# A one-column product written as a scalar-tensor-tensor operation, and a row minimum that starts from the sink's column

## The chip, the cores and the metric

The kernel runs on one core of one Trainium2 chip. The core has five engines that work side by side and wait for one another through semaphores: TensorE (PE in the profile, its weight loads PEld), VectorE (DVE), ScalarE (ACT), GpSimd (POOL), and SyncE (SP), which here only issues DMA transfers. The metric is the device time of one execution in microseconds (us); lower is better. Each engine carries out its own list of instructions in order.

## The reference

One layer of a decoder: RMSNorm, two attention branches side by side, gates, a residual, a second RMSNorm, a gated MLP with a width-3 causal convolution, a residual and a last RMSNorm, on 1024 tokens of 1024 channels, all in float32. The two branches matter here.

The first is differential attention with 4 heads. Each head has two query/key components of 64 channels, and the result uses the difference of two softmaxes:

```python
logits = s - slopes[:, None, None, None] * dist
logits = jnp.where(dist >= 0, logits, NEG_INF)
p = jax.nn.softmax(logits, axis=-1)
a = p[:, :, 0] - lam * p[:, :, 1]
return jnp.einsum('bhqs,bshe->bqhe', a, v)
```

The second is sliding-window attention, 8 heads in 2 groups, a window of 128, in which each head has a learned sink: one more logit that takes part in the softmax and has no value behind it:

```python
p = jax.nn.softmax(jnp.concatenate([logits, sink], axis=-1), axis=-1)[..., :-1]
o = jnp.einsum('bnkgqs,bnskd->bnqkgd', p, vw)
```

## The kernel before, in words

Activations lie transposed, with channels on the 128 partitions and tokens in the free dimension. Most products are made to float32 accuracy from three passes: a float32 operand is split into a high and a low part, and TensorE adds high x high, high x low and low x high into one PSUM bank. `mm3` (lines 150 to 152) and `product` (835 to 837) are those passes; the splits are copies on ScalarE and subtractions on VectorE (lines 129 and 131 for weights, 755 and 756 for activations).

The stages follow one another: `project` (all input projections, up to about 250 us), `attention` (to about 500 us), `rest` (gates, the merging of the branches, `mix`), `hidden` (the up projection and the convolution) and `down`.

`attention` has six units `u`. Units 0 to 3 are the heads of the differential attention, each of 8 blocks of 128 queries (`da_step`); units 4 and 5 are the two groups of the sliding window, each of 8 blocks for four heads at once (`sw_step`). Between the blocks stand `back_half` calls: half a gate projection each, 24 matmuls of 512 columns that depend on nothing in the attention (lines 150 to 152 and the copy on line 497). They fill TensorE while a softmax is on its way.

A block of the first kind does, for each of two components: scores on TensorE (line 568) into PSUM; on VectorE one operation that adds the bias, scales, writes the negated logits and keeps their minimum along the row (line 572, shown in the profile as CUSTOM_DVE_ANT_0, followed by a DVE_READ_ACCUMULATOR2_ANT that writes the minimum out); on ScalarE the exponential with that minimum as bias and the row sum as second output (line 573). Then the reciprocal of one sum (576), a product of one column (577), the combination of the two components (578), transposes of the result on TensorE (584), their copy to a high part (586, ScalarE) and a low part (587, VectorE), and the product with the values (596 to 598).

A block of the second kind does, for four heads: scores (656), the bias-scale-minimum operation for each head (659), the minimum of the four columns with the four negated sinks (661), the sum with the sinks (662) and its exponential (663), four exponentials of the scores with the minimum as bias (665), the addition of the sink's term (666), the reciprocal (667), the scaling of the four heads (670: three on VectorE, the fourth on GpSimd), transposes (677), the split (680 and 681), the product with the values (687), and a copy and two additions (689 and 694) before the store.

After the attention `rest` reads the stored results back (`yr`, line 712), splits them (755 and 756) and multiplies them with the output weights of the branches; these are the first products that need everything from the attention.

The order of the instructions on each engine isn't written out by hand. A list scheduler of the framework puts every engine's instructions in order, by its own estimate of what each costs and of when its inputs are there. A changed instruction can therefore move others, on all engines.

The calls that the change touches are in `da_step` and `sw_step`. The column `self.neglam` is minus lambda, `self.nsink` holds the eight negated sinks, and `self.s0` the row sums of the first component.

Of the kernel before, what the change touches and what calls it, by code (L numbers as in the profile page):

```python
# [13 lines left out]
ALU = mybir.AluOpType  # L14
# [28 lines left out]
class Trunk:  # L43
# [510 lines left out]
    def da_step(self, h, i, st, aT):  # L554
        nc, ap = self.nc, self.ap
        q, k = st
        slope = 4.0 ** -(h + 1)
        w = (i + 1) * P

        lo = P if w == 640 else 0  # L560
        cuts = ((0, 256),) if i == 0 else ((0, w),) if w <= H2 else ((0, H2 - lo), (H2 - lo, w))
        pr = []
        for c in range(2):
            sc = self.tl(self.psS, [P, T], "sc")
            qs = q[c][:, i * P:(i + 1) * P]
            for part in range(2):
                for n0, n1 in cuts:
                    nc.tensor.matmul(sc[:, lo + n0:lo + n1], qs, k[c][part][:, n0:n1], start=part == 0, stop=part == 1)  # L568
            L = self.tl(ap, [P, T], "L", bufs=4)
            s = self.tl(self.st, [P, 4], "sm", bufs=8)  # L570
            o = 896 - i * P
            nc.vector.tensor_tensor_reduce(L[:, :w], sc[:, lo:lo + w], self.bias[:, o:o + w], slope, 3e38, ALU.add, ALU.min, s[:, 0:1])  # L572
            nc.scalar.activation(L[:, :w], L[:, :w], AF.Exp, bias=s[:, 0:1], scale=-1.0, accum_out=s[:, 1:2] if c else self.s0[:, i:i + 1])  # L573
            pr.append(L)

        nc.vector.reciprocal(s[:, 2:3], s[:, 1:2])
        nc.vector.tensor_scalar(s[:, 3:4], self.s0[:, i:i + 1], s[:, 2:3], self.neglam, ALU.mult, ALU.mult)
        nc.vector.scalar_tensor_tensor(pr[0][:, :w], pr[1][:, :w], s[:, 3:4], pr[0][:, :w], ALU.mult, ALU.add)
        qo = (i % 2) * P
        for j0 in range(0, i + 1, 4):  # L580
            nj = min(4, i + 1 - j0)
            ps = self.tl(self.psT, [P, 4, P], "t")
            for j in range(nj):
                nc.tensor.transpose(ps[:, j, :], pr[0][:, (j0 + j) * P:(j0 + j + 1) * P], self.ident)
            hi, lo = aT[j0 // 4, 0], aT[j0 // 4, 1]
            nc.scalar.copy(hi[:, :nj, qo:qo + P], ps[:, :nj, :])
            nc.vector.tensor_tensor(lo[:, :nj, qo:qo + P], ps[:, :nj, :], hi[:, :nj, qo:qo + P].bitcast(F32), ALU.subtract)
# [57 lines left out]
    def sw_step(self, g, n, st):  # L645
        nc, ap = self.nc, self.ap
        q, k = st
        k0 = max(n - 1, 0) * P
        w = P if n == 0 else 256
        bo = T + (P if n == 0 else 0)  # L650
        sc = self.tl(self.psS, [P, 4, 256], "sc")
        s = self.tl(self.st, [P, 4, 4], "sw", bufs=4)
        L = self.tl(ap, [P, 4, 256], "L", bufs=4)
        for h in range(4):
            for part in range(2):
                nc.tensor.matmul(sc[:, h, :], q[h][:, n * P:(n + 1) * P], k[part][:, k0:k0 + 256], start=part == 0, stop=part == 1)
        for h in range(4):
            slope = 2.0 ** -(4 * g + h + 1)
            nc.vector.tensor_tensor_reduce(L[:, h, :w], sc[:, h, :w], self.bias[:, bo:bo + w], slope, 3e38, ALU.add, ALU.min, s[:, 0, h:h + 1])
        sink = self.vecs[:, C_SINK + 4 * g:C_SINK + 4 * g + 4]  # L660
        nc.vector.tensor_tensor(s[:, 0, :], s[:, 0, :], self.nsink[:, 4 * g:4 * g + 4], ALU.min)
        nc.vector.tensor_tensor(s[:, 1, :], s[:, 0, :], sink, ALU.add)
        nc.scalar.activation(s[:, 1, :], s[:, 1, :], AF.Exp)
        for h in range(4):
            nc.scalar.activation(L[:, h, :w], L[:, h, :w], AF.Exp, bias=s[:, 0, h:h + 1], scale=-1.0, accum_out=s[:, 2, h:h + 1])
        nc.vector.tensor_tensor(s[:, 2, :], s[:, 2, :], s[:, 1, :], ALU.add)
        self.last = nc.vector.reciprocal(s[:, 3, :], s[:, 2, :])
        for h in range(4):
            eng = nc.gpsimd if h in (3,) else nc.vector
            eng.tensor_scalar(L[:, h, :w], L[:, h, :w], s[:, 3, h:h + 1], None, ALU.mult)  # L670
        po = self.tl(self.psT, [P, H2], "t")
        nblk = w // P
        parts = []
        for b in range(nblk):
            ps = self.tl(self.psT, [P, 4, P], "t")
            for h in range(4):
                nc.tensor.transpose(ps[:, h, :], L[:, h, b * P:(b + 1) * P], self.ident)
            pt = self.tl(ap, [P, 2, 4, P], "aT", F32R, bufs=5)
            hi, lo = pt[:, 0], pt[:, 1]
            nc.scalar.copy(hi, ps)  # L680
            nc.vector.tensor_tensor(lo, ps, hi.bitcast(F32), ALU.subtract)
            parts.append((hi, lo))
        for b, (hi, lo) in enumerate(parts):
            kb = k0 // P + b
            va = self.vsw[kb // 4][:, kb % 4, g]
            for m, pt in enumerate((hi, lo)):
                nc.tensor.matmul(po, va, pt, start=b == 0 and m == 0, stop=b == nblk - 1 and m == 1)
        t = self.tl(self.gpool, [P, 4, P], "g", bufs=2)[0:64]
        nc.scalar.copy(t, po[64:128].rearrange("p (h q) -> p h q", h=4))
        pv = po[0:64].rearrange("p (c e q) -> p c e q", c=2, e=2)  # L690
        tv = t.rearrange("p (c e) q -> p c e q", e=2)
        y = self.tl(ap, [P, 2, P], "ys", bufs=3)
        for e in range(2):
            nc.vector.tensor_tensor(y[64 * e:64 * e + 64], pv[:, :, e], tv[:, :, e], ALU.add)
        self.store(self.yd[4 + 2 * g:6 + 2 * g, :, n * P:(n + 1) * P].rearrange("c p q -> p c q"), y)
# [515 lines left out]
```

## Time and profile before

| quantity | value |
|---|---|
| median of 3 runs | 1355.06 us (1354.48 to 1355.87) |
| profiled execution | 1356.2 us, of which the span of instructions 1354.3 us |
| TensorE busy | 1335.0 us, 99% of the span |
| VectorE busy | 1009.8 us, 75% |
| ScalarE busy | 603.9 us, 45% |
| GpSimd busy | 483.1 us, 36% |
| mean granted TensorE clock | 0.996 |

The profile is taken by the hardware profiler in one execution. Its page gives the busy time of each engine, the span in 40 slices, the chain of work that ended last, and groups of instructions by line with their mean duration and the idle time ahead of them. Other views are cut from the same execution: the waits (who waited for whom and for how long), a table of stretches of the span, and the timeline, in which a row is a start, a duration, an engine, a line, an operation, its output and inputs, and in square brackets the idle time ahead of it with what ended it. Matmuls are pipelined: each is shown for longer than the distance to the next, so a TensorE that is shown as busy isn't proof of full speed. The waits of the weight loads (PEld) show short stops better.

### The profile page before, as it was taken

To read this page: it belongs to the slowest core of one execution; us is meant where nothing else is said; L and a number is where in the kernel's file an instruction comes from. 1 tells how busy PE (TensorE), PEld (TensorE's weight loads), DVE (VectorE), ACT (ScalarE), POOL (GpSimd) and SP (SyncE) were. 2 spreads that over 40 slices of the span, in tenths; PEclk is the share of its full clock that TensorE was granted. 3 is DMA by queue.
4 is the path that set the end of the run, shared out by engine and by line. 5 is a ranking of instruction groups with operands and counts; after the bars stand their busy time and mean duration, and the time that the engine had idled before them with its cause. 6 is when DMAs were issued, how large, how long until landed. Compare 5 with 4: busy or idle time off the path is not lost.

```text
span 1354.3 us, 17160 instructions
## 1 busy us (share of the span) xinstructions
PE 1335.0 (99%) x6304; PEld 1103.6 (81%) x6304; DVE 1009.8 (75%) x1454; ACT 603.9 (45%) x942; POOL 483.1 (36%) x350
## 2 busy tenths in 40 slices
PE   7999999999999999999999999999999999999997
PEld 6888888888887777878888888888888888888886
DVE  8846775388898875355689888888888898986454
ACT  8422232376667664334444334433443345433343
POOL 0436651010102125741455565555555611231011
PEclk9999999999999999999999999999999999999999
DMA  6334443966554235334422222122212248651342
GB/s 255 140 113 164 143 156 114 272 174 175 156 133 144 77 116 219 117 119 136 166 82 88 71 91 94 62 79 93 93 63 83 92 141 311 215 177 64 94 134 85
DMA packets 62470, 179.50 MB, mean 133 GB/s; under 512 B 6833, under 2 KB 15153, under 8 KB 62385
## 3 DMA queue, kind: packets, MB, share of 16 engines
q1 hardware_dynamic: 50928, 160.98, 36.7%
q10 hardware_dynamic: 11456, 17.41, 3.5%
q8 instruction: 50, 0.82, 0.2%
q14 instruction: 36, 0.29, 0.1%
HBM read 129.61 MB, written 48.76 MB: 132 GB/s over the span
## 4 chain that ended last, share of the span: by engine, by line
PE 62%; DVE 17%; POOL 7%; issue 7%; DMA 4%; ACT 3%; POOLq 0%; DVEq 0%; SPq 0%; ACTq 0%
PE t L836 7%; PE t L837 7%; PE t L835 7%; POOL us L965 3%; PE y L996 3%; PE d L996 3%; PE sc L568 3%; PE g L150 2%; PE g L151 2%; DVE c L958 2%; PE g L152 2%; DVE wl L112 2%; DMA gr<-gd 2%; PE sc L151 2%; PE sc L152 2%
## 5 line engine op out<-in xcount | busy, mean ns | idle before, releaser
L970 ACT ACTIVATE c<-us,vecs 128x1024 f32<-128x1024 f32 x44 | 54.8, 1248 | 163.2 <-POOL us L965 160.0
L965 POOL TENSOR_TENSOR us<-us,rstd 128x1024 f32<-128x1024 f32 x42 | 100.7, 2414 | 52.8 <-DVE wl L131 34.3
L110 ACT CAST sh<-sf 128x1024 fp32r<-128x1024 f32 x62 | 64.9, 1051 | 106.2 <-POOL sf L97 61.8
L129 ACT CAST wh<-raw 128x1024 fp32r<-128x1024 f32 (+2 forms) x60 | 60.7, 1012 | 104.8 <-PE sc L151 33.1
L971 DVE SCALAR_TENSOR_TENSOR c<-us,vecs,c 128x1024 f32<-128x1024 f32 x44 | 67.1, 1527 | 51.9 <-ACT c L970 51.9
L131 DVE TENSOR_TENSOR wl<-raw,wh 128x1024 fp32r<-128x1024 f32 (+2 forms) x60 | 75.3, 1256 | 39.1 <-ACT wh L129 29.3
L96 POOL TENSOR_TENSOR sf<-rv 128x512 f32<-128x512 f32 x30 | 42.5, 1417 | 166.7 <-DMA rv<-in_w_up 73.2
L112 DVE TENSOR_TENSOR sl<-sf,sh 128x1024 fp32r<-128x1024 f32 x62 | 88.3, 1426 | 8.2 <-ACT sh L110 8.2
L167 POOL TENSOR_TENSOR rs<-ms,mhalf 128x8 f32<-128x8 f32 (+2 forms) x9 | 14.5, 1614 | 159.1 <-DVE ms L165 148.5
L150 PE MATMUL g<-xh,wh 128*128 128x512 f32 x176 | 70.7, 402 | 0.1
L152 PE MATMUL g<-xh,wl 128*128 128x512 f32 x176 | 70.4, 400 | 0.0
L151 PE MATMUL g<-xl,wh 128*128 128x512 f32 x176 | 70.4, 400 | 0.0
L98 POOL TENSOR_TENSOR sf<-raw,rv 128x512 f32<-128x512 f32 x30 | 41.6, 1386 | 59.9 <-DVE sl L112 59.9
L572 DVE CUSTOM_DVE_ANT_0 L<-sc,bias 128x128 f32<-128x128 f32 (+7 forms) x64 | 47.7, 752 | 17.4 <-PE sc L568 14.1
L551 POOL MEMSET aT<- 128x128 f32 x32 | 6.1, 204 | 152.0 <-PE t L597 101.6
L573 ACT ACTIVATE L<-L,sm 128x128 f32<-128x128 f32 (+7 forms) x64 | 49.6, 778 | 20.7 <-DVE sm L572 18.2
L97 POOL TENSOR_TENSOR sf<-sf,raw 128x512 f32<-128x512 f32 x31 | 58.0, 1870 | 1.6
L972 DVE SCALAR_TENSOR_TENSOR c<-us,vecs,c 128x1024 f32<-128x1024 f32 x44 | 56.2, 1279 | 0.6
L725 POOL TENSOR_TENSOR gr<-gr,rstd 128x1024 f32<-128x1024 f32 x16 | 39.4, 2467 | 41.4 <-DMA gr<-gd 41.2
L112 DVE TENSOR_TENSOR wl<-raw,wh 128x1024 fp32r<-128x1024 f32 (+1 forms) x35 | 52.8, 1508 | 0.1
L151 PE MATMUL sc<-ml,wh 128*128 128x512 f32 x128 | 50.1, 391 | 0.6 <-DVE ml L746 0.6
L568 PE MATMUL sc<-u,u 128*128 128x512 f32 (+2 forms) x192 | 49.8, 359 | 0.1
(444 smaller groups left out, 4351.4 us busy)
## 6 DMA issues: line engine op xcount, KB each, us to landing
u<-qd SPq DMA_DIRECT2D x72, 256.0 KB, 6.1
raw<-in_w_down SPq DMA_DIRECT2D x27, 512.0 KB, 3.7
raw<-in_w_in SPq DMA_DIRECT2D x25, 512.0 KB, 4.4
hr<-hd SPq DMA_DIRECT2D x50, 256.0 KB, 5.3
raw<-in_w_up SPq DMA_DIRECT2D x23, 512.0 KB, 3.6
hd<-c SPq DMA_DIRECT2D x22, 512.0 KB, 2.8
rv<-in_w_up SPq DMA_DIRECT2D x21, 512.0 KB, 3.5
gr<-gd SPq DMA_DIRECT2D x16, 512.0 KB, 3.6
```

What stands on the lines that cost most here:

```text
L112: nc.vector.tensor_tensor(lo, src, hi.bitcast(F32), ALU.subtract)
L131: self.lo = (eng or nc.vector).tensor_tensor(wl, raw, wh.bitcast(F32), ALU.subtract)
L150: nc.tensor.matmul(ps, wh[:, kc + o, :], ah, start=first and n == 0, stop=False)
L151: nc.tensor.matmul(ps, wh[:, kc + o, :], al, start=False, stop=False)
L152: nc.tensor.matmul(ps, wl[:, kc + o, :], ah, start=False, stop=last and n == len(kcs) - 1)
L568: nc.tensor.matmul(sc[:, lo + n0:lo + n1], qs, k[c][part][:, n0:n1], start=part == 0, stop=part == 1)
L835: nc.tensor.matmul(ps, ah[:, k, :], bh, start=first and n == 0, stop=False, skip_group_check=skip)
L836: nc.tensor.matmul(ps, ah[:, k, :], bl, start=False, stop=False, skip_group_check=skip)
L837: nc.tensor.matmul(ps, al[:, k, :], bh, start=False, stop=last and n == len(ks) - 1, skip_group_check=skip)
L965: i = (nc.vector if m % NF == 0 else nc.gpsimd).tensor_tensor(us[:, 2:], us[:, 2:], self.rstd, ALU.mult)
L971: nc.vector.scalar_tensor_tensor(c, us[:, 1:T + 1], cw[1], c, ALU.mult, ALU.add)
L996: nc.tensor.matmul(ps, v[:, n, :], x, start=n == i == 0, stop=n == len(js) - 1 and i == 2)
```

## The change

Two edits. In `da_step` the one-column product on line 577, a tensor-scalar operation whose two factors are both columns given as pointers, becomes a scalar-tensor-tensor operation: one factor is a pointer (`self.neglam`), the other (`s[:, 2:3]`) is a tensor of one column. In `sw_step` the minimum of each head starts from the column of the negated sink instead of from the constant 3e38, so the separate minimum on line 661 goes.

```diff
         nc.vector.reciprocal(s[:, 2:3], s[:, 1:2])
-        nc.vector.tensor_scalar(s[:, 3:4], self.s0[:, i:i + 1], s[:, 2:3], self.neglam, ALU.mult, ALU.mult)
+        nc.vector.scalar_tensor_tensor(s[:, 3:4], self.s0[:, i:i + 1], self.neglam, s[:, 2:3], ALU.mult, ALU.mult)
         nc.vector.scalar_tensor_tensor(pr[0][:, :w], pr[1][:, :w], s[:, 3:4], pr[0][:, :w], ALU.mult, ALU.add)
...
         for h in range(4):
             slope = 2.0 ** -(4 * g + h + 1)
-            nc.vector.tensor_tensor_reduce(L[:, h, :w], sc[:, h, :w], self.bias[:, bo:bo + w], slope, 3e38, ALU.add, ALU.min, s[:, 0, h:h + 1])
+            nc.vector.tensor_tensor_reduce(L[:, h, :w], sc[:, h, :w], self.bias[:, bo:bo + w], slope, self.nsink[:, 4 * g + h:4 * g + h + 1], ALU.add, ALU.min, s[:, 0, h:h + 1])
         sink = self.vecs[:, C_SINK + 4 * g:C_SINK + 4 * g + 4]
-        nc.vector.tensor_tensor(s[:, 0, :], s[:, 0, :], self.nsink[:, 4 * g:4 * g + 4], ALU.min)
         nc.vector.tensor_tensor(s[:, 1, :], s[:, 0, :], sink, ALU.add)
```

## The prediction

> **What bounds the kernel now.** I read the page first: the busy times, then the chain that ended last.
>
> ```profile
> span 1354.3 us, 17160 instructions
> PE 1335.0 (99%) x6304; PEld 1103.6 (81%) x6304; DVE 1009.8 (75%) x1454; ACT 603.9 (45%) x942; POOL 483.1 (36%) x350
> PE 62%; DVE 17%; POOL 7%; issue 7%; DMA 4%; ACT 3%; POOLq 0%; DVEq 0%; SPq 0%; ACTq 0%
> ```
>
> TensorE is all but never idle and leads the chain, so an edit on VectorE is worth only what it takes from, or adds to, TensorE's stops. Next the table of stretches: differential attention up to 396, sliding window 396 to 500, hand-over to the output projections 500 to 520.
>
> ```profile
> core 0: us, PE busy (x) PEld busy (x) DVE busy (x) ACT busy (x) POOL busy (x), PEclk, DMA share, GB/s
> 250.00:300.00 50.00, 49.91 (x283) 42.41 (x283) 34.09 (x92) 28.95 (x70) 1.55 (x8) 1.00 0.83 216
> 300.00:396.00 96.00, 95.92 (x618) 84.38 (x616) 83.78 (x212) 65.66 (x151) 9.26 (x25) 1.00 0.55 149
> 396.00:500.00 104.00, 102.17 (x569) 82.42 (x568) 88.05 (x319) 71.42 (x209) 17.53 (x18) 1.00 0.38 115
> 500.00:520.00 20.00, 19.55 (x84) 15.00 (x83) 14.35 (x12) 13.43 (x15) 8.12 (x4) 1.00 0.77 288
> ```
>
> VectorE is 87% busy in 300 to 396 (83.78 of 96) and 85% in 396 to 500, next behind TensorE; the clock is full. The stops themselves are in the waits of the weight loads, here of 396 to 500 (line, what it waited for, total us, times, longest).
>
> ```profile
> PEld t L687 <- DVE aT L681: 3.6, 11, 0.6
> PEld t L677 <- issue: 1.8, 6, 0.4
> PEld t L677 <- DVE L L670: 1.3, 6, 0.3
> PEld t L677 <- PE t L687: 0.5, 1, 0.5
> PEld t L677 <- ACT g L497: 0.5, 1, 0.5
> PEld t L677 <- ACT aT L680: 0.4, 1, 0.4
> PEld t L677 <- POOL L L670: 0.4, 1, 0.4
> ```
>
> These are 8.5 us, of which 4.9 stand in front of the transposes (line 677), the end of the softmax chain, and 3.6 in front of the product with the values. So the whole stake of the sliding-window edit is some 8 to 9 us out of 1355, and 0.2% of the time, which is about what a measurement of this kernel can tell from no change, is 2.7 us.
>
> **The change part by part.** VectorE first, by rows of the timeline, since distances between starts are what an operation takes from the engine, and by groups (busy us, mean ns of one, idle before).
>
> ```profile
> 311.39 0.27 DVE L577 TENSOR_SCALAR sm<-s,sm,neglam 128x1 f32<-128x1 f32 x1
> 311.58 0.95 DVE L572 CUSTOM_DVE_ANT_0 L<-sc,bias 128x768 f32<-128x768 f32 x1
> 427.69 0.42 DVE L659 CUSTOM_DVE_ANT_0 L<-sc,bias 128x256 f32<-128x256 f32 x1
> 429.76 0.15 DVE L661 TENSOR_TENSOR sw<-sw,nsink 128x4 f32<-128x4 f32 x1
> 429.83 0.42 DVE L659 CUSTOM_DVE_ANT_0 L<-sc,bias 128x256 f32<-128x256 f32 x1
> 430.71 0.50 ACT L665 ACTIVATE L<-L,sw 128x256 f32<-128x256 f32 x1
> 433.15 0.51 ACT L665 ACTIVATE L<-L,sw 128x256 f32<-128x256 f32 x1
> ```
>
> ```profile
> L577 DVE TENSOR_SCALAR sm<-s,sm,neglam 128x1 f32<-128x1 f32 x32 | 8.7, 271 | 0.3
> L661 DVE TENSOR_TENSOR sw<-sw,nsink 128x4 f32<-128x4 f32 x16 | 2.5, 158 | 0.1
> L578 DVE SCALAR_TENSOR_TENSOR L<-L,sm,L 128x384 f32<-128x384 f32 x4 | 2.5, 620 | 0.1
> L578 DVE SCALAR_TENSOR_TENSOR L<-L,sm,L 128x256 f32<-128x256 f32 x4 | 1.9, 484 | 0.1
> ```
>
> *The product, 32 times.* Line 577 lasts 271 ns and holds the engine for 0.19 us (311.39 to 311.58). No one-column form of the new operation is in the trace. Its nearest rows are line 578: (620 - 484) / 128 is 1.06 ns a column, so 484 - 256 x 1.06 leaves 212 ns for one column. From below the 158 ns of line 661 (no pointer) bounds it, from above the old 271. I take 212, the row of the same operation: 59 ns less, 1.9 us of VectorE over 32 blocks. The blocks' end is TensorE, which has few stops there, so most of it is hidden; if that cover went, all 1.9 us would count. Taken: -0.3, ends -1.9 and 0.
>
> *The minimum, 16 times.* It lasts 158 ns but the next operation starts 0.07 us after it (429.76 to 429.83): 16 x 0.07 = 1.1 us leave VectorE. The Trainium skill's page "VectorE: DVE Perf Modes", section "Rules for kernel authors", says not to fuse for its own sake, since the pipeline is flushed behind every operation, and to make fewer operations. By a full flush the gain would be the durations, 16 x 0.158 = 2.5 us, and the sum below would come out about 0.5 us lower (the 1.4 us more, by the same share of VectorE's change that I take for the path); the two starts 0.07 us apart speak against a full flush here.
>
> *The pointer, 64 times.* The bias-scale-minimum operation now reads a column. The nearest price is line 577 against line 661: 0.19 - 0.07 = 0.12 us for two pointers, 0.06 for one. 64 x 0.06 = 3.8 us; the lower end is 0, where it hides behind the stream of 256 columns, the upper end 64 x 0.12 = 7.7 if one costs what two do. I take 0.06: it is the same engine and the same size of column. With the minimum gone VectorE has 2.7 us more to do in a stage where it is 85% busy (-1.1 to +6.6). VectorE's free 16 us hide some; taken: +1.0 on the path, ends -1.1 and +4.
>
> *The waits.* Before, none of a block's four exponentials could start until all four minima and line 661 were done. In the rows above the last of a block's four starts at 427.69; line 661 comes 2.07 us later, behind other work in VectorE's queue, and the block's exponentials only follow then (430.71 is still the block ahead; 433.15 is this block's third). Now each exponential waits for its own minimum. A chain that is free to run gains line 661 with its queueing and up to three exponentials at 0.5 us, less 4 x 0.06 for the pointers: about 1.4 to 3 us a block.
>
> *The order.* The changed kernel was built, and its instruction order stands beside the old. Nothing moves before about 255 us or behind the hand-over. What a matmul takes of TensorE is read from the chain in order of time (start, us, what), and two rows of the timeline show how close the transposes follow their inputs.
>
> ```profile
> 439.11 0.44 PE t L677 x4
> 439.55 0.95 PE sc L656 x8
> 441.65 0.23 PE g L152
> ```
>
> ```profile
> 450.40 0.67 DVE L670 TENSOR_SCALAR L<-L,sw 128x128 f32<-128x128 f32 x3
> 450.90 0.30 PE L677 MATMUL t<-ident,L 128*128 128x128 f32 x1 [0.16 <-DVE L L670]
> ```
>
> So a matmul of 128, 256 and 512 columns takes 0.11, 0.12 and 0.23 us. At these, TensorE's work between a block's last score matmul and its first transpose, counted in both orders, shrinks in the window stage by 1.0 us a block on average (late blocks: 8.3 to 6.6, 11.2 to 10.0, 8.3 to 7.2, 7.6 to 6.2, 12.5 to 10.7, 9.9 to 8.8). The scheduler has thus spent most of the shorter chain in advance. I put what remains at half of the 4.9 us in front of line 677: -2.5. Ends: -4.9, and +2.4, where the chain falls 0.6 us short in each of 8 tight blocks (two blocks are in flight, and a stop serves both: half of 8 x 0.6). In the first branch the same room grows by 0.6 us a block, and that between transposes and their use changes by under 0.25 us where it is short: nothing taken.
>
> *The hand-over.* Here the order changes most.
>
> ```profile
> 501.98 3.90 ACT L755 CAST yh<-yr 128x1024 fp32r<-128x1024 f32 x4 [0.41 <-ACT g L497]
> 506.19 1.05 ACT L129 CAST wh<-raw 128x1024 fp32r<-128x1024 f32 x1 [0.32 <-PE g L151]
> 514.16 1.05 ACT L755 CAST yh<-yr 128x1024 fp32r<-128x1024 f32 x1 [0.83 <-DMA yr<-yd]
> 515.38 1.05 ACT L755 CAST yh<-yr 128x1024 fp32r<-128x1024 f32 x1 [0.17 <-DMA yr<-yd]
> 509.21 1.21 DVE L131 TENSOR_TENSOR wl<-raw,wh 128x1024 fp32r<-128x1024 f32 x1
> 515.24 2.45 DVE L756 TENSOR_TENSOR yl<-yr,yh 128x1024 fp32r<-128x1024 f32 x2 [0.66 <-ACT yh L755]
> 517.79 0.45 PE L151 MATMUL g<-yl,wh 128*128 128x512 f32 x1
> ```
>
> The cast of the second weights (506.19) moves behind the seventh `yh` cast, in front of the eighth, and its low part (509.21) in front of the last `yl`. The eighth `yh` then ends at 515.38 + 2 x 1.05 = 517.5 in place of 516.4, the last `yl` at 516.5 + 2 x 1.21 = 518.9 in place of 517.7, so 1.2 us later. TensorE takes its first matmul with it at 517.79, as soon as it is there. In the old order five matmuls of the next product stand ahead of that point, in the new one only one, so TensorE has less to fill the time with and comes out one matmul (0.23 us) further behind. Taken +1.4; ends 0, where the transfers of `yr` land earlier than before, and +2. On SP one weight load goes behind three transfers of stacks and another behind an input load; both weights are loaded ahead of the product before theirs (`ahead`), so I take nothing; without that lead the gate matmuls would stop.
>
> *Sum:* -0.3 + 1.0 - 2.5 + 1.4 = -0.4 us. The profiled execution took 1356.2 us, 1.9 more than its span and 1.1 above the median; against the median of 1355.06 the forecast is 1354.7.
>
> **The rivals.** *A, slower: the room is cut and the chain doesn't follow.* Place: lines 670 to 677 in the window stage. ScalarE's in-order queue may have other work in front of the exponentials, as the gap between 430.71 and 433.15 shows. In the 8 tight blocks the room is cut by 1.6 us on average; where the chain gets less than that shorter, it decides. Against it: 2.07 us lay between a last minimum and line 661 alone. Price as above: +2.4 in place of -2.5, so +4.5, 1359.6. *B, faster: the chain gains more than the cut everywhere and the pointer hides.* All 4.9 us in front of line 677 go: -4.9 - 0.3 + 1.4 = -3.8, 1351.3. Against it: the late blocks' transposes already start right behind their inputs (450.40 and 450.90) with the larger room. *C, the edit does nothing:* the waits simply move from line 677 to 687, whose split stays as it is; then -0.3 + 1.0 + 1.4 = +2.1, 1357.2, still inside 0.2%.
>
> **How the numbers follow.** Forecast and C together 0.47 (the forecast 0.32), A 0.31, B 0.22. These are also same, slower and faster. The likeliest case's own range is 1352.4 to 1357.7. For 8 in 10 the range reaches past B's time and to A's with the dearer pointer: 1349.5 to 1360.5.
>
> **What would show it.** Right: line 659 near 0.48 us for 256 columns (0.42 now), line 577 near 0.21, line 661 gone, the waits of line 677 down by some 2 us, the last `yl` about 1.2 us later after the first output matmul, and everything before 255 us and behind 520 us as it was. Wrong: waits of line 677 above 5 us (A), near zero (B), a line 659 above 0.5 us, or a stop in front of the gate matmuls (lines 150 to 152) for late weights, which I have put at nothing.

## The result and the profile after

The changed kernel takes 1358.87 us (median of 13 runs, 1356.48 to 1360.61) where the kernel before took 1355.87 us in runs beside it (1354.48 to 1357.76). The ratio is 1.0021, with a 95% interval of 1.0013 to 1.003: some 2.9 us slower. Measured twice more, each time beside other runs below, it came out at 1.0016 and 1.0019. The profiled execution took 1358.49 us.

The head of the page, and two groups of VectorE (busy us, mean ns of one, idle before), of the kernel after:

```profile
span 1356.5 us, 17141 instructions
PE 1335.2 (98%) x6304; PEld 1103.9 (81%) x6304; DVE 1012.9 (75%) x1438; ACT 604.3 (45%) x942; POOL 482.9 (36%) x350
```

```profile
L659 DVE CUSTOM_DVE_ANT_0 L<-sc,bias,nsink 128x256 f32<-128x256 f32 x56 | 25.2, 473 | 0.6 <-PE sc L656 0.6
L577 DVE SCALAR_TENSOR_TENSOR sm<-s,neglam,sm 128x1 f32<-128x1 f32 x32 | 6.9, 215 | 0.4
```

The instructions cost what the prediction gave them: the one-column product 215 ns (212 said), the pointer 473 - 418 = 55 ns (60 said), with line 659's old mean of 418 ns as the group of `x1_stt` below shows it. VectorE's busy time on the page rises by 3.1 us (1012.9 - 1009.8), but that is not the edits alone: the kernel before shows 1011.1 us in a second execution, and 1.6 us of the rise stand in the eight low parts `yl` behind the attention, one of which took 3.42 us in this execution (below). TensorE has the same work. Behind line 660 the changed kernel's line numbers are one lower than before: 676, 686 and 755 are the old 677, 687 and 756.

To see where the 2.9 us arise I take four marks from the starts of TensorE's matmuls. In the rows of one line (count, min/median/max ns, first and last start us, shapes) these are the first score product of the first branch (568), the first of the sliding window (656), the last product with its values (687), and the first output product (line 150 with `yh`; `yh` and `yl` are the high and the low part of the attention's stored results, lines 755 and 756). Before:

```profile
L568 PE MATMUL sc<-u,u x192: 277/365/493, 256.4 to 389.8; 128*128 128x512 f32 x80, 128*128 128x256 f32 x64, 128*128 128x384 f32 x48
L656 PE MATMUL sc<-u,u x128: 275/283/383, 390.3 to 480.6; 128*128 128x256 f32 x128
L687 PE MATMUL t<-aT,v x60: 387/396/505, 410.5 to 497.6; 128*128 128x512 f32 x60
L150 PE MATMUL sc<-yh,wh x64: 388/390/397, 506.2 to 588.6; 128*128 128x512 f32 x64
```

After:

```profile
L568 PE MATMUL sc<-u,u x192: 274/368/501, 257.0 to 389.3; 128*128 128x512 f32 x80, 128*128 128x256 f32 x64, 128*128 128x384 f32 x48
L656 PE MATMUL sc<-u,u x128: 274/283/368, 392.0 to 483.0; 128*128 128x256 f32 x128
L686 PE MATMUL t<-aT,v x60: 387/395/501, 412.1 to 498.0; 128*128 128x512 f32 x60
L150 PE MATMUL sc<-yh,wh x64: 388/389/398, 507.1 to 592.0; 128*128 128x512 f32 x64
```

The first branch takes 390.3 - 256.4 = 133.9 us before and 392.0 - 257.0 = 135.0 after, so 1.1 more. The window stage takes 497.6 - 390.3 = 107.3 and 498.0 - 392.0 = 106.0, so 1.3 less. The gap to the first output product grows from 8.6 to 9.1, because two more gate matmuls stand behind the last product with the values (39 in place of 37); one was taken out of each of the two stages. Together the attention loses 0.3 us. The output products then spread over 592.0 - 507.1 = 84.9 us in place of 82.4: 2.5 us lost in this execution, of which the rest of the program gave 1.2 back.

The waits of the weight loads show what TensorE waited for (line, what for, total us, times, longest). First branch, 250 to 396, before:

```profile
PEld sc L568 <- DVE sm L572: 1.4, 7, 0.2
...
PEld t L584 <- ACT y L599: 0.8, 3, 0.3
```

and after:

```profile
PEld sc L568 <- DVE sm L572: 3.4, 13, 0.4
PEld t L584 <- ACT y L599: 1.6, 6, 0.3
```

A score product waits for a PSUM buffer that VectorE still has to read, 13 times instead of 7. Window stage, 396 to 500, after:

```profile
PEld g L150 <- ACT g L497: 2.3, 3, 1.8
PEld t L676 <- DVE L L669: 2.0, 9, 0.3
PEld t L686 <- ACT aT L679: 1.3, 6, 0.4
PEld t L676 <- PE t L686: 1.3, 2, 1.0
PEld t L686 <- DVE aT L680: 0.9, 4, 0.3
```

With rows of 0.2 and 0.3 us counted too, the waits in front of the transposes (676) are 3.5 us in place of 5.1, those in front of the product with the values (686) 2.2 in place of 3.9, and those of gate matmuls for line 497 grow from 0.3 to 2.3. Hand-over and gates, 500 to 600, before and after:

```profile
PEld sc L151 <- DVE yl L756: 1.4, 3, 0.6
...
PEld g L151 <- DVE yl L756: 0.7, 2, 0.5
```

```profile
PEld g L151 <- DVE yl L755: 3.3, 3, 2.1
PEld g L150 <- ACT yh L754: 1.0, 2, 0.7
PEld sc L151 <- DVE yl L755: 0.5, 1, 0.5
```

TensorE waited 2.1 us for low parts before and 3.8 after.

### The profile page after: what moved, and what is told of

It reads as the page before. It is cut to its first block, busy times and chain, and to the rows that moved or that the text cites. A ratio compares the mean times of both kernels' runs of the same rounds, so it can differ in the third digit from the quotient of the medians.

```text
span 1356.5 us, 17141 instructions
## 1 busy us (share of the span) xinstructions
PE 1335.2 (98%) x6304; PEld 1103.9 (81%) x6304; DVE 1012.9 (75%) x1438; ACT 604.3 (45%) x942; POOL 482.9 (36%) x350
## 4 chain that ended last, share of the span: by engine, by line
PE 44%; DVE 9%; issue 4%; POOL 2%; ACT 1%; DMA 1%; POOLq 0%; DVEq 0%
PE t L836 6%; PE t L835 6%; PE t L834 6%; PE y L995 3%; PE d L995 3%; PE sc L151 3%; PE sc L152 3%; PE sc L150 3%; POOL us L964 2%; PE d L1022 2%; PE y L1022 2%; DVE wl L112 1%; DVE c L957 1%; PE g L151 1%; PE g L152 1%
```

## The experiments

In all kernels below the lines bear the numbers of the kernel before. "First branch", "window" and "gap" are the three distances just read, as differences to the kernel before in us; "behind" is the rest, from the first output product to the last matmul of the program. Each is read from the starts of matmuls in one profiled execution; the start of the first branch itself scatters by up to 0.9 us between executions, and is left out.

| run | edits | ratio (95%) | first branch | window | gap | behind |
|---|---|---|---|---|---|---|
| changed kernel | both | 1.0021 (1.0013 to 1.003) | +1.1 | -1.3 | +0.5 | +1.4 |
| after_again | both | 1.0016 (1.0007 to 1.0025) | +1.2 | -1.3 | +0.5 | +1.7 |
| after_third | both | 1.0019 (1.001 to 1.0028) | +1.1 | -1.3 | +0.5 | +2.8 |
| before_again | none | 1.0001 (0.9992 to 1.0009) | -0.1 | 0 | 0 | +1.1 |
| p1_early | first | 1.003 (1.0019 to 1.0042) | +1.2 | +2.4 | +0.3 | +0.2 |
| p2_early | second | 1.0008 (0.9999 to 1.0017) | 0 | -2.9 | +1.1 | +4.0 |
| x1_stt | first, old order | 0.9999 (0.999 to 1.0008) | -0.1 | -0.1 | 0 | +2.6 |
| x2_old | none, order of p1_early | 1.0033 (1.0022 to 1.0045) | +1.5 | +2.7 | +0.2 | -0.1 |
| x3_both | both, old order | 1.0006 (0.9996 to 1.0015) | -0.3 | +0.5 | 0 | +1.1 |
| x3_again | both, old order | 1.0005 (0.9996 to 1.0014) | -0.2 | +0.6 | 0 | +1.1 |
| d_late | none, late weight | 1.0017 (1.0009 to 1.0026) | -0.1 | -0.1 | 0 | +2.8 |
| x6_late | both, old order, late weight | 1.0019 (1.001 to 1.0028) | -0.2 | +0.6 | 0 | +2.7 |
| c_early | both, early weight | 1.0019 (1.001 to 1.0028) | +1.2 | -1.3 | +0.5 | +2.8 |
| c_again | both, early weight | 1.0014 (1.0005 to 1.0023) | +1.3 | -1.3 | +0.5 | +2.0 |
| e_pool | both, GpSimd held | 1.002 (1.0011 to 1.0029) | +1.2 | -1.2 | +0.5 | +1.4 |
| x4_try | both, order of p2_early | 1.0025 (1.0016 to 1.0034) | -0.3 | -2.9 | +1.1 | +4.6 |

The attention's distances repeat within 0.2 us for one order of instructions. What lies behind does not: for the kernel before it is 0 and 1.1 in two executions, for the changed kernel 1.4, 1.7 and 2.8. And `x1_stt` shows +2.6 there in an execution of 1359.09 us, where its median is 1356.39. So there the medians have to decide: the difference of the medians less the three distances is 2.7, 2.1 and 2.2 us for the changed kernel, and I call this "behind by the medians".

**The same kernels again.** The kernel before as it is:

> The kernel before, unchanged, run as the others are, for a second profile and as the zero of the comparison. All theories: 0.0 against before (within 0.7 us). Theory N (each program that isn't the one measured first comes out about 2.5 us longer, whatever is in it): +2.5. Theory R (the loss lies behind the first output product, in the loop of the gates): its stretch from the first output product to the last product of the mix is as short as in the first profile, 176.5 us, within 0.5; if it is 1 to 2 us longer, the first profile was a lucky one there and the difference of the profiles says less than the medians.

Ratio 1.0001: two copies of one program can't be told apart. The changed kernel as it is:

> The changed kernel once more, on the same chip as the three others, for its time beside theirs and a second profile: +2.9 us against before (0.2%). If the front of the program (0.85 us of the profiled difference before the attention begins) and the 1.1 us in the first branch are chance, they differ in this profile; the 2.5 us between the first and the last of the output products must be there again.

1.0016. Its last low part `yl` took 1.23 us in this execution, not the 3.4 us of the first profile (below), and the kernel is as slow as before: that meeting isn't what makes it slow.

**The hand-over.** The changed kernel casts the second output weight late. `d_late` moves only this cast, in the kernel before; `c_early` moves it back, in the changed one. (The cast comes with taking the weight, `next_w`, and goes early again when the first sigmoid is queued behind the last `yh`.)

```diff
 # d_late, against the kernel before (y6: the cast of the seventh yh)
-                    w = self.next_w()
+                    with tc.issue_after(y6.ins) if m == 0 else nullcontext(): w = self.next_w()
 # c_early, against the changed kernel
-                        with tc.issue_after(self.hi.ins) if br else nullcontext():
+                        with tc.issue_after(self.hi.ins) if br or m == 0 else nullcontext():
```

> The kernel before, with one thing moved: ScalarE casts the second output weights behind the seventh yh cast (as the changed kernel's order has it) and not ahead of the sigmoid. Theory H (the loss is made at the hand-over: the last yl is 1.2 us later, and, since it then meets GpSimd's gate product, takes 3.4 us in place of 1.2): slower than before by 2.5 us (1.8 to 3.2), with the last yl above 3 us. Theory S (the loss comes from the softmax edits and the new order around them): same as before within 0.7 us. Theory C (only the cast's place counts, the meeting with GpSimd costs nothing): +1.2.

> The changed kernel with one more dependency: the first sigmoid of the gates is issued after the cast of the second output weights, which restores the old order at the hand-over and moves nothing else. Theory H: 2.5 us below the changed kernel, so +0.5 against before (-0.5 to +1.2). Theory S: as the changed kernel, +2.9 against before.

The kernel before with a late weight comes out at 1.0017, and taking the late weight back in the changed kernel saves nothing (1.0019). So a late weight is enough for such a loss, and not needed for it. In `d_late` a wait for the weight itself appears (500 to 600):

```profile
PEld sc L150 <- ACT wh L129: 2.3, 1, 2.3
```

None of the changed kernel's three profiles has this wait, and the order tells why. `d_late` has the changed kernel's order on ScalarE, but not on TensorE and VectorE. The first matmul with the late weight, in the changed kernel and then in `d_late`, where the low part of the weight (line 131) also comes behind the last `yl` and not in front of it:

```profile
519.08 0.39 PE L150 MATMUL sc<-yh,wh 128*128 128x512 f32 x1
```

```profile
516.80 0.50 PE L150 MATMUL sc<-yh,wh 128*128 128x512 f32 x1 [1.84 <-ACT wh L129]
```

So `d_late` is a late weight in another order than the changed kernel's. `c_early` is the cleaner of the two: behind the attention it has the order of the kernel before on all engines.

In the first profile of the changed kernel the stop had another owner. From its timeline (start, us, engine, line):

```profile
515.44 1.22 DVE L755 TENSOR_TENSOR yl<-yr,yh 128x1024 fp32r<-128x1024 f32 x1 [1.01 <-ACT yh L754]
...
517.59 5.80 POOL L724 TENSOR_TENSOR gr<-gr,rstd 128x1024 f32<-128x1024 f32 x2 [12.46 <-DMA gr<-gd]
...
517.72 3.42 DVE L755 TENSOR_TENSOR yl<-yr,yh 128x1024 fp32r<-128x1024 f32 x1
```

The last `yl` began 0.13 us after a gate product on GpSimd (`gr`, line 724 here, 725 before) and took 3.42 us instead of 1.22; this is the 2.1 us wait of line 151 above. `e_pool` holds GpSimd's third gate product back until the last `yl` is done:

```diff
                         i = nc.gpsimd.tensor_tensor(g, g, self.rstd, ALU.mult)
+                        if m == 1: tc.add_manual_dep(i.ins, last_yl.ins.name, mybir.DependencyInfo(mybir.DependencyClass.Sync, mybir.DependencyReason.DATA), reason="port")
```

> The changed kernel, in which GpSimd's third gate product waits for the last yl, so that the two no longer run at the same time; the casts stay in the changed order. Theory H: the last yl takes 1.2 us again, the kernel is 1.5 to 2.2 us below the changed one, +0.7 to +1.4 against before. Theory C: as the changed kernel, +2.9. Theory S: as the changed kernel, +2.9.

The last `yl` takes 1.22 us again, and the ratio is 1.002. The meeting is a matter of one execution, not the cause.

**The edits apart.** Both kernels keep the early weight, so that only the attention differs.

```diff
 # p1_early: line 577 changed, lines 659 and 661 as before
+        nc.vector.scalar_tensor_tensor(s[:, 3:4], self.s0[:, i:i + 1], self.neglam, s[:, 2:3], ALU.mult, ALU.mult)
 # p2_early: line 577 as before, line 659 with self.nsink, line 661 gone
```

> The first edit alone (the one-column product), with the old order at the hand-over held by the extra dependency. Theory S1 (the first branch loses 1.1 us by its new order, whatever else happens): first score matmul of the window stage 1.1 us later, counted from the first score matmul of the attention, and the time +1 or more against before. Theory R (all attention effects cancel, the loss comes behind): as c_early, +3.0. Neither: 0.

> The second edit alone (the minimum that begins with the sink's column), with the old order at the hand-over held by the extra dependency. The window stage should be 0.8 us shorter as in the changed kernel, and the first branch as before: without a loss behind, -0.8 against before. Theory R (a loss behind the first output product in whatever differs from before): +1.5 to +3.

The first edit, which makes VectorE's work shorter by 1.8 us, costs 3.6 us within the two stages of the attention. The second wins 2.9 us in the window stage, 1.1 of them by gate matmuls that move behind it into the gap, and is still no faster: 1.0008. In its hand-over two `yl` met GpSimd, as in the first profile.

**The order held fast.** An edit that makes an operation 56 ns shorter can't cost 3.6 us by its duration. But the scheduler, whose estimate of the instruction changes, gives all engines a new order. So I separated the two: each kernel's instructions are chained, engine by engine, in the recorded order of another, with edges that set the order of issue and make nothing wait.

```diff
-            self.rest(gctx)
+            self.rest(gctx); pin(nc, tc)
...
+def pin(nc, tc):
...
+            if prev is not None:
+                tc.add_manual_dep(body[at], prev.name, mybir.DependencyInfo(mybir.DependencyClass.NoSync, mybir.DependencyReason.DATA), reason="order")
+            prev = body[at]
```

`x1_stt` is the first edit in the order of the kernel before; `x2_old` is the kernel before, not one instruction changed, in the order of `p1_early`; `x3_both` has both edits in the order of the kernel before, with the 16 minima left out. The traces show each engine in the recorded order.

> The first edit alone (the one-column product as a scalar-tensor-tensor operation), with every instruction of the program held in the order in which the kernel before issues it on its engine. The first edit in its own order lost 1.18 us in the first branch and 2.41 us in the window stage against before. Theory O (the loss is the new order that the edit brings, not the instruction): both stages as in before, within 0.2 us (first branch slightly better, up to -0.3 us, for the 60 ns of each of 32 products), and a time within 0.1% of before (ratio 0.999 to 1.001). Theory I (the instruction itself costs, by its latency to the next operation): first branch +0.8 to +1.3 us again, ratio 1.0005 to 1.0015.

> The kernel before, none of its instructions changed, held in the issue order that the first edit alone got (with the hand-over's weight in its old place). Theory O: first branch +1.0 to +1.4 us and window stage +2.2 to +2.6 us, as the first edit alone had, ratio 1.0015 to 1.004. Theory I: both stages within 0.3 us of before, ratio 0.9995 to 1.0005.

The marks of `x1_stt`, then those of `x2_old`:

```profile
L568 PE MATMUL sc<-u,u x192: 274/365/492, 257.1 to 390.4; 128*128 128x512 f32 x80, 128*128 128x256 f32 x64, 128*128 128x384 f32 x48
L656 PE MATMUL sc<-u,u x128: 277/283/385, 390.8 to 481.1; 128*128 128x256 f32 x128
L687 PE MATMUL t<-aT,v x60: 387/395/505, 411.1 to 498.0; 128*128 128x512 f32 x60
```

```profile
L568 PE MATMUL sc<-u,u x192: 274/368/506, 257.0 to 389.7; 128*128 128x512 f32 x80, 128*128 128x256 f32 x64, 128*128 128x384 f32 x48
L656 PE MATMUL sc<-u,u x128: 274/282/387, 392.4 to 483.0; 128*128 128x256 f32 x128
L687 PE MATMUL t<-aT,v x60: 387/395/505, 411.8 to 502.5; 128*128 128x512 f32 x60
```

The new instruction in the old order takes 133.7 and 107.2 us, no more than before; the old instruction in the new order takes 135.4 and 110.1. The waits of the first branch say the same, of `x1_stt` first and of `x2_old` second:

```profile
PEld sc L568 <- DVE sm L572: 1.0, 5, 0.2
```

```profile
PEld sc L568 <- DVE sm L572: 3.5, 13, 0.4
```

Both stages even lose 0.1 us more than theory O allowed. The loss of `p1_early` in the attention is the order, and none of it the instruction. In the new order 146 of the first branch's 192 score matmuls have fewer gate matmuls ahead of them than before; TensorE asks for the score buffer before VectorE has read it. One chip, one set of runs: 0.9999 against 1.0033.

> Both edits, the 16 minima gone, everything held in the order of the kernel before. It measures the window softmax's instructions without a new order: 64 pointer operands at 57 ns (+3.6 us of VectorE) against 16 minima at about 70 ns from start to start (-1.1 us). Theory P (VectorE's balance sets the stage, the gain seen came from the new order): window stage +1 to +2.5 us, first branch 0 to -0.3 us, ratio 1.0005 to 1.002. Theory M (a link less in each chain is worth more than the pointers cost, order apart): window stage -0.5 to -3 us, ratio 0.998 to 0.9997. In both the hand-over has its old order.

Both edits in the old order take 0.5 us more in the window stage, where `x1_stt` took 0.1 less, so the second edit costs 0.7 us there by its instructions. A group and the window stage's waits of `x3_both` show how:

```profile
L659 DVE CUSTOM_DVE_ANT_0 L<-sc,bias,nsink 128x256 f32<-128x256 f32 x56 | 25.0, 478 | 1.7 <-PE sc L656 1.7
```

```profile
PEld t L687 <- DVE aT L681: 3.9, 12, 0.6
PEld t L677 <- issue: 1.8, 6, 0.4
PEld t L677 <- DVE L L670: 1.5, 6, 0.3
PEld sc L656 <- DVE sw L659: 1.1, 2, 0.6
```

Set against the prediction's rows, the waits for line 670 and line 681 have not shrunk (1.3 to 1.5, 3.6 to 3.9) although line 661 is out of the chain. `x1_stt`, with line 661 still there, has 1.3 and 3.6 too. Its group first, then its waits:

```profile
L659 DVE CUSTOM_DVE_ANT_0 L<-sc,bias 128x256 f32<-128x256 f32 x56 | 21.7, 418 | 1.6 <-PE sc L656 1.6
```

```profile
PEld t L687 <- DVE aT L681: 3.6, 11, 0.6
...
PEld t L677 <- DVE L L670: 1.3, 6, 0.3
PEld sc L656 <- DVE sw L659: 0.6, 2, 0.4
```

Of the 18 stops for lines 670 and 681 in `x3_both`, 15 end with an operation that VectorE began within 0.03 us of its last one; for the other three, all in front of line 681, it first waited for ScalarE's copy (680). So it is mostly not the chain from the scores to the transposes that ends these stops, but VectorE, which reaches the two lines when it has worked through its queue, and the queue is longer by the pointers. So in the window stage theory P has the sign right, and +1 as its lower end was too dear: the gain that the changed kernel shows there, 1.3 us, came with its new order (1.8 to 1.9 us better than the same instructions in the old one), 0.2 us of it by one gate matmul fewer in the stage. Whether the old instructions would gain as much in that order is not shown: no run holds them in it.

**Can the second edit's order be kept?** `x4_try` holds both edits in the order of `p2_early`, and holds GpSimd's first two gate products behind the fourth and the eighth `yl`, so that none meets one.

```diff
+                            tc.add_manual_dep(i.ins, (last_yl if br else yl4).ins.name, mybir.DependencyInfo(mybir.DependencyClass.Sync, mybir.DependencyReason.DATA), reason="port")
```

> Both edits, held in the order that the second edit alone got (window stage -2.95 us there, first branch -0.05), and GpSimd's first two gate products held back behind the 4th and the 8th low half of the attention's output, so that no low half runs beside one (two of them took 3.4 us there instead of 1.2, and the stop before the fourth product of the gates was 2.5 us). Theory O with the collision as the rest of the loss: first branch 0, window stage -2.9 us of which 1.2 us come back behind it as moved gate work, no low half over 1.4 us, products of the hand-over within 1 us of before, ratio 0.998 to 0.9995. If the ratio is over 1, what the attention wins is lost in the hand-over whatever GpSimd does.

The first four `yl` take 4.63 us here. In `p2_early` they took 9.02 beside GpSimd. From the two timelines, `p2_early` first:

```profile
500.95 9.02 DVE L756 TENSOR_TENSOR yl<-yr,yh 128x1024 fp32r<-128x1024 f32 x4 [4.20 <-ACT yh L755]
...
501.90 5.85 POOL L725 TENSOR_TENSOR gr<-gr,rstd 128x1024 f32<-128x1024 f32 x2 [12.63 <-DMA gr<-gd]
```

```profile
501.28 4.63 DVE L756 TENSOR_TENSOR yl<-yr,yh 128x1024 fp32r<-128x1024 f32 x4 [4.18 <-ACT yh L755]
...
506.05 3.46 POOL L725 TENSOR_TENSOR gr<-gr,rstd 128x1024 f32<-128x1024 f32 x1 [16.44 <-DVE yl L756]
```

The time gained went into later gate products, which now come late from GpSimd (waits of `x4_try`, 500 to 600):

```profile
PEld g L150 <- DVE gr L741: 4.0, 4, 1.1
PEld g L150 <- ACT yh L755: 1.2, 1, 1.2
```

1.0025, against 1.0008 for `p2_early` on another chip (`x4_try` also has the first edit, which cost nothing in `x1_stt`): holding GpSimd is dearer than the meetings were. No version that I ran beats the kernel before.

**The rest of the loss.** The changed kernel reaches its first output product 0.3 us later than before, yet ends 2.2 to 2.9 us later. Four kernels of the same instructions on one chip: attention in the old or the new order, hand-over with the early or the late weight. `x6_late` is `x3_both` in the recorded order of `d_late`, so its late weight stands as there and not as in the changed kernel; it too waits for the weight (1.4 us for line 129 and 2.0 for line 131).

> Both edits in the order of the kernel before, a second time, as the corner of a square: attention in the order of before, hand-over in the order of before. Theory A (the new order of the attention and the new order of the hand-over each cost by themselves, and add): ratio 1.0000 to 1.001. Theory E (either one alone costs all that there is to lose, by taking the hand-over's slack): the same. First branch -0.3, window stage +0.5 us, as in its first run.

> Both edits, attention in the changed kernel's order, hand-over in the order of the kernel before (its first run: ratio 1.0019). Theory A: 1.0005 to 1.0012 (the 0.3 us that the attention's order loses by the time of the first output product, and what lies between), so its first run was high. Theory E: 1.0015 to 1.0025, as much as the changed kernel itself. First branch +1.15, window stage -1.3 us.

> Both edits, attention in the order of before, hand-over's weight late, in the order that the kernel before got when its weight alone was moved (ratio 1.0017 there). Theory A: 1.0017 to 1.0025. Theory E: 1.0015 to 1.0025 too; a ratio under 1.001 would say that the late weight costs nothing of its own. First branch -0.3, window stage +0.5 us.

> The changed kernel again, beside the three others on the same chip. Theory A: the sum of what the two orders cost alone over the first corner. Theory E: no more than the dearer of the two, 1.0015 to 1.0025.

| | early weight | late weight |
|---|---|---|
| attention in the old order | 1.0005 (1.0006 in the first run) | 1.0019 |
| attention in the new order | 1.0014 (1.0019 in the first run) | 1.0019 (1.0021, 1.0016) |

On the early side the square is clean, and it holds the main result: with the same instructions and the hand-over's order of the kernel before, the attention's new order takes the ratio from 1.0005 to 1.0014 (from 1.0006 to 1.0019 in the first runs, which were on two chips). The intervals of a pair overlap, but both pairs say the same. The changed kernel, at 1.0016 to 1.0021, can't be told from `c_early` and `c_again`: its late weight costs nothing that could be measured on top.

With the late side taken as it is, either new order costs about 0.1%, both together no more than one. If they added, the last corner would be at 1.0028 (1.0005 + 0.0009 + 0.0014) by these runs and at 1.0032 by the first ones; its three values lie at 1.0016 to 1.0021. That speaks for theory E without proving it: each ratio is known to some 0.0009 only, so a sum of three is less sure still, and the two late corners have different late orders. The column "behind" points the same way: the two kernels that reach the output products latest (`p1_early` and `x2_old`, +3.9 and +4.4 us by their three distances) lose nothing after that (0.0 and 0.2 by the medians), the two that reach them earliest (`p2_early` and `x4_try`, -1.8 and -2.1) lose 4.0 and 4.6 (3.1 and 5.1 by the medians; in `x4_try` GpSimd was held). This suggests that the pace of the hand-over is to a good part set not by TensorE's arrival but by what feeds it: transfers of `yr` and `gr`, GpSimd, ScalarE, VectorE. Which link is late in the new attention order isn't settled: in `c_early` it was the gate products (2.2 us in front of line 150 for line 741), in other executions the `yl`.

## Why the prediction was right or wrong

*The time.* Forecast 1354.7, which is 0.4 us less than before; measured 1358.87, some 3 us more than the 1355.87 beside it: inside the stated range, on the wrong side. (The range's upper end is not what the terms give: A with the pointer at its upper end of +4 would be 1362.6, not 1360.5.) "Slower" had 0.31, for rival A; but A's mechanism isn't what happened, since the waits in front of the transposes fell to 3.5 us where A needed more than 5. (Within them, those for line 670 did rise, from 1.3 to 2.0.)

*The prices on VectorE* were right: 212 ns said and 215 measured for the product, 60 and 55 to 60 ns for a pointer. With the starts 0.07 us apart for the 16 minima, these give VectorE 2.4 to 2.7 us more in the window stage, where 2.7 was said; the page's +3.1 for the whole program has other parts in it and is no check. The forecast's "+1.0 on the path" for the window stage became 0.7 in the old order (`x3_both` against `x1_stt`).

*The product, -0.3:* the first branch has -0.1 to -0.3 in the three executions with the old order (`x1_stt`, `x3_both`, `x3_again`), and -0.1 in `before_again`. That fits, at the edge of what can be read.

*The waits, -2.5:* this step failed. It took the chain through the four minima and line 661 to end half of the waits in front of line 677. With the order held, the shorter chain took nothing off them (`x3_both`: 4.8 us of 5.1 are left, and the waits for VectorE's scaling went from 1.3 to 1.5). In the new order they fell by 1.6 us, but that goes with the order: `p2_early` and the changed kernel differ by 1.6 us in this stage, with the same second edit.

*The order in the first branch, "nothing taken":* this step failed as well, and cost 1.1 us. I had looked only at the room between a block's last score product and its first transpose, which grows. It grows because score products move forward, and the buffer that they need is then still unread: 13 stops of 3.4 us in place of 7 of 1.4. The window stage's 1.3 us made up for it, so at the first output product the changed kernel was only 0.3 us late; most of its loss arose behind that.

*The hand-over, +1.4:* the sign was right, but by luck, since the step failed. The changed kernel does lose 2.1 to 2.7 us behind the first output product (by the medians), but `c_early` and `c_again`, which have the weight early, lose 2.7 and 1.6 there all the same. The last `yl` doesn't explain it either: it began 10.57, 10.46 and 11.18 us after the first output product in three executions of the changed kernel and 10.25 and 10.73 in two of the kernel before, so not 1.2 us later as forecast, and in `c_early` and `c_again` it began at 10.19 and 10.17. The transfers of `yr` had landed up to 1.2 us earlier in two of the three; I had that as the lower end. What a late weight can cost, `d_late` shows in an order of its own: 2.3 to 2.8 us (0.17% of 1356, and its "behind"), where +2 was the upper end. Its biggest stop, 2.3 us on the weight itself, is one that the prediction named as a sign of error and had put at nothing: it counted when the weight is loaded, not when its cast is done. In the changed kernel's three profiles that stop doesn't show. That the terms may not add was not thought of.

*The sum by the runs:* the instructions of both edits together about +0.7 us (1.0005 and 1.0006, with intervals that take in 1), which is what the forecast's two terms for them add up to, -0.3 and +1.0. The rest, some 2 us, came with the new order; the attention's part of that order is by `c_early` and `c_again` enough for most of it. So the terms that failed are those for the order: the waits, the first branch, and what happens behind the attention. Why the attention's new order costs most of its time only behind the first output product stays open.

## What to carry to other kernels

When a scheduler orders the engines, a change of one instruction is two changes: the instruction and the order. Hold the order and change the instruction, then change the order and hold the instruction; here the first gave 0.9999 and the second 1.0033. Before counting on a shorter chain, look at which engine's queue ends the wait: where VectorE is 85% busy, a pointer operand of 55 to 60 ns on 64 operations outweighs 16 small operations saved (+0.7 us in that stage with the order held). And look behind the stage that you change: here two versions came 1.8 and 2.1 us earlier out of the attention and kept none of it.

## What the runs showed of the hardware

A subtraction on VectorE with both inputs in SBUF took 3.38 to 3.46 us in place of 1.21 to 1.23 when it began while a GpSimd product of the same size was running. The other way round GpSimd loses: in the kernel before, its third gate product began 0.2 us after the last `yl` (516.67 after 516.47 us) and took 3.28 us in place of 2.41, and the `yl` took no longer than the others. In the rows of the changed kernel above, the first product, which began before the `yl`, took 2.45 us, and the second, which began while the `yl` was at work, 3.39. The Trainium skill, page "SBUF — State Buffer", section "Who interferes with whom", says that such an operation contends with a GpSimd instruction that reads SBUF; the trace agrees. The Trainium skill's same page, section "SBUF: two separate sides", says that whichever of the two starts first holds an exclusive lock and that the other fully blocks. The trace agrees with that too: VectorE's 2.2 us more are almost the 2.41 us of a product, and GpSimd's 0.9 us more almost what was left of the `yl`.
